# One 128-column stationary operand for the two halves of v, and an add by VectorE

## The chip, the cores and the metric

The kernel runs on one core of one Trainium2 chip. The metric is the device time of one execution in microseconds; the figure quoted for a kernel is the median of its runs.

## The reference, cut to what matters

Two transformer blocks run one after the other on 512 tokens of width 1024. The change touches the second block alone: a mixer with four groups of four attention heads of width 64 (A, dilated causal; B, stick-breaking; C, a band of 128 with sinks, two heads of values shared by four of queries; D, causal over blocks), and a cross attention of four heads over 256 memory tokens. In all of them the output of a head is a product of a weight matrix with that head's values:

```python
# softmax heads (A, C, D and cross attention), for each head:
p = exp(score + bias - max) / denominator
y = p @ v                       # v: keys x 64
# stick-breaking heads (B): p comes from sigmoids and a running sum of softplus, y = p @ v as well
```

## The kernel before, in words

Activations lie transposed, features on the 128 partitions and the tokens along a row. A product of two float32 matrices is made from float32r halves: each operand is split into a high half (a ScalarE copy) and a low half (a VectorE subtraction), and three matmuls are accumulated, high by high, high by low and low by high (`split`, `mm3`).

`hybrid` runs the mixer. Its list `plan` pairs the heads of a group (`heads`, `band_heads`) with jobs that fill TensorE meanwhile: the projections of the next groups (`pair`, `values`) and the output projection (`project_out`). `weave` starts one generator per tile of 128 queries and moves all running ones one step on, then emits some of the fill. The order within each engine's queue is set when the program is built, from simulated times of the instructions (`schedule_with_timeline_sim=True`); each engine then runs its queue in that order. The plan goes B, A, D, C; `cross` follows with the same softmax generators and its own fill.

A softmax generator (`softmax_units`, `unit`) handles 128 queries: two score matmuls (line 1206) into a bank `sc`, minimum or maximum and exponential, normalisation, transposes of the weights by TensorE (line 1228) into a bank `tr`, and their split into pth and ptl, which hold two query tiles side by side, 256 columns. After the second tile of a pair come the products with v (lines 1250 to 1254): for each block of 128 keys that both tiles see one block of 256 columns, for the others one of 128 columns; three matmuls each, whose stationary operand is the 64 columns of one head in v's high or low half (tiles v2h, v2l; xv in cross attention). They fill rows 0 to 63 of a `tr` bank, and ScalarE copies these to the head's rows of y, rows 0 to 63 or 64 to 127.

A stick-breaking generator (`stick_units`) handles 128 keys and all later queries, so its products (line 1307) have 512, 384, 256 and 128 columns; four generators of a head accumulate in one `tr` bank, copied at the end (line 1310).

There are three `tr` banks, shared by transposes, half of the stick-breaking scores and these outputs.

The values come from `values` (line 1418; groups A, B and D by tiles of 128 tokens, group C by transposing a projection) and, for cross attention, from `memory_keys` (line 1598) early in the kernel; that one writes its halves to HBM (`mvd`) over SP's queue, and `memory_load` (line 1642) fetches them on GpSimd's queue at the start of `cross`.

Of the kernel before, what the change touches and what calls it, by code (L numbers as in the profile page):

```python
# [63 lines left out]
class Net:  # L64
# [1114 lines left out]
            out.append((kh, kl))  # L1179
        return out  # L1180

    def softmax_units(self, q, ks, v, vc, y, yr, window, bias=None, sink=None, keys=SEQ, tag=lambda pair: pair,
                      again=False):

        nc = self.nc
        V = nc.vector
        vh, vl = v
        nkt = keys // P  # L1190
        st = {}

        def unit(ti):
            pair, i = divmod(ti, 2)
            wins = [window(2 * pair + n) for n in range(2)]
            k0, k1 = wins[i]
            f0 = wins[0][0]
            w = (k1 - k0) * P
            if bias is not None and (ti == 0 or again and i == 0):
                st["e"] = self.bt.tile([P, 512], FT, name="bias")  # L1200
                nc.sync.dma_start(st["e"], bias)
            ps = self.psc.tile([P, 512], FT, name="sc")
            qs, q0 = q(pair)
            qs = qs[:, q0 + i * P:q0 + i * P + P]
            for x in range(2):
                nc.tensor.matmul(ps[:, 0:w], qs, ks[x][:, k0 * P:k1 * P], start=x == 0, stop=x == 1)
            p = self.at.tile([P, keys], FT, name="e")[:, 0:w]
            nm, den = (self.at.tile([P, 1], FT, name=n) for n in ("nm", "den"))
            if bias is not None:
                o = 384 - P * ti + P * k0  # L1210
                V.tensor_tensor_reduce(p, ps[:, 0:w], st["e"][:, o:o + w], -1.0, 3.0e38 if sink is None else sink[1],
                                       OP.add, OP.min, nm)
            else:
                V.tensor_reduce(nm, ps[:, 0:w], AX.X, OP.max, negate=True)
                nc.scalar.activation(p, ps[:, 0:w], AF.Exp, bias=nm, accum_out=den)
            yield
            if bias is not None:
                nc.scalar.activation(p, p, AF.Exp, scale=-1.0, bias=nm, accum_out=den)
            if sink is not None:
                e = self.at.tile([P, 1], FT, name="es")  # L1220
                nc.scalar.activation(e, sink[0], AF.Exp, bias=nm)
                V.tensor_tensor(den, den, e, OP.add)
            V.reciprocal(den, den)
            V.tensor_scalar(p, p, den, None, OP.mult)
            yield
            pt = self.ptr.tile([P, 512], FT, name="tr")
            for j in range(k1 - k0):
                nc.tensor.transpose(pt[:, j * P:(j + 1) * P], p[:, j * P:(j + 1) * P], self.ident)
            yield
            if i == 0:  # L1230
                n = wins[1][1] - f0
                k = tag(pair)
                full = 1280 if k and keys == SEQ else 512
# [12 lines left out]
            both = [j for j in range(nkt) if a0 <= j < a1 and b0 <= j < b1]  # L1246
            jobs = [(j, 0, 256) for j in both]
            jobs += [(j, 0, P) for j in range(a0, a1) if j not in both]
            jobs += [(j, P, 256) for j in range(b0, b1) if j not in both]
            for ji, (j, c0, c1) in enumerate(jobs):  # L1250
                for x, (m, d) in enumerate(((vh, pth), (vh, ptl), (vl, pth))):
                    nc.tensor.matmul(yp[0:64, c0:c1], m[:, j, vc:vc + 64], d[:, j - f0, c0:c1], start=ji == x == 0,
                                     stop=ji == len(jobs) - 1 and x == 2)
            nc.scalar.activation(y[yr, pair * 256:pair * 256 + 256], yp[0:64, 0:256], AF.Copy)

        return [unit(i) for i in range(4)]

    def stick_units(self, q, ks, v, vc, y, yr):


        nc = self.nc
        V, G = nc.vector, nc.gpsimd
        vh, vl = v
        st = {}

        def unit(i):
# [36 lines left out]
            if i == 3:  # L1303
                st["y"] = self.ptr.tile([P, 512], FT, name="tr")
            yp = st["y"]
            for x, (m, d) in enumerate(((vh, ah), (vh, al), (vl, ah))):
                nc.tensor.matmul(yp[0:64, t0:SEQ], m[:, i, vc:vc + 64], d, start=i == 3 and x == 0,
                                 stop=i == 0 and x == 2, skip_group_check=True)
            if i == 0:
                nc.scalar.activation(y[yr], yp[0:64], AF.Copy)  # L1310

        return [unit(i) for i in (3, 2, 1, 0)]

# [28 lines left out]
    def hybrid(self):  # L1342
# [3 lines left out]
        with ExitStack() as es:  # L1346
# [65 lines left out]

            def new_v(name):
                pool = self.vx if name == "D" else self.vp
                boxes[name]["v"] = tuple(pool.tile([P, 4, 256], FR, name=n) for n in ("v2h", "v2l"))
                return boxes[name]["v"]

            def values(name):

                if name == "C":  # L1420
                    def then(vf):
                        vh, vl = new_v("C")
                        pt = self.ptr.tile([P, 512], FT, name="tr")
                        for j in range(4):
                            nc.tensor.transpose(pt[:, j * P:(j + 1) * P], vf[:, j * P:(j + 1) * P], self.ident)
                        self.split(vh[:, :, 0:P], vl[:, :, 0:P], pt.rearrange("p (a b) -> p a b", a=4))
                    return pair(15, 1.0, then)
                ws = []

# [3 lines left out]
                                           ready=self.ready.get(("v", "ABD".index(name), c))) for c in range(2))  # L1433

                def tile_(t):
                    vh, vl = boxes[name]["v"]
                    ps = self.pmm.tile([P, 512], FT, name="mm")
                    sl = slice(NM + t * P, NM + t * P + P)
                    self.mm3(ps[:, 0:256], [(self.xh[k][:, sl], self.xl[k][:, sl], ws[k // 4][0][:, k % 4, :],
                                             ws[k // 4][1][:, k % 4, :]) for k in range(KT)])  # L1440
                    col = self.rcol[HALF[t // 2][0]]
                    self.split(vh[:, t, :], vl[:, t, :], ps[:, 0:256], col[:, t % 2:t % 2 + 1])
                return load, [lambda t=t: tile_(t) for t in range(4)]

            def finish(g):
# [31 lines left out]
            def heads(name, j):  # L1477
                def gens():
# [5 lines left out]
                    for i in range(2):  # L1484
                        h = 2 * j + i
                        y, yr, q = ys[2 * g + j], slice(64 * i, 64 * i + 64), box["q", j][i]
                        if name == "B":
                            yield from self.stick_units(q, box["k", j][i], box["v"], 64 * h, y, yr)
                            continue
                        e = self.bias_tile({"A": 0, "D": 8}[name] + h)  # L1490
                        yield from self.softmax_units(lambda pair, q=q: (q, 256 * pair), box["k", j][i], box["v"],
                                                      64 * h, y, yr, causal, e)
                return gens

            def band_heads(pair):

                box = boxes["C"]
                if pair == 0:
                    for j in range(2):
                        ys[4 + j] = bt.tile([P, SEQ], FT, name="qkn")  # L1500
                    for h in range(4):
                        j, i = divmod(h, 2)
                        q = box["q", j][i]
                        box["u", h] = self.softmax_units(
                            lambda pair, q=q: (q, 256 * pair), box["k", 0][j], box["v"], 64 * j, ys[4 + j],
                            slice(64 * i, 64 * i + 64), band, self.bias_tile(4 + h),
                            (self.par[:, sk + h:sk + h + 1], nsink[:, h:h + 1]),
                            tag=lambda pair, h=h: 1 if pair else h % 2, again=True)
# [89 lines left out]
    def memory_keys(self, mp):  # L1598
# [2 lines left out]
        nc = self.nc  # L1601
        mh, ml, rm = self.mem
        self.mkd = self.dram.tile([P, 8, MEM], FT, name="mkd")
        self.mvd = self.dram.tile([P, 4, 256], FT, name="mvd")

        def keys(f):
            st = {}
# [14 lines left out]
                            nc.sync.dma_start(self.mkd[o:o + 64, 4 * f + 2 * j + x],  # L1622
                                              ks[x][64 * j:64 * j + 64].bitcast(FT))
            return load, [make]
        v = [mp.tile([P, 2, 256], FR, name=n) for n in ("vh", "vl")]
        ws = []

        def load():
# [2 lines left out]
        def values(t):  # L1631
# [1 line left out]
            sl = slice(t * P, t * P + P)  # L1633
            self.mm3(ps[:, 0:256], [(mh[k][:, sl], ml[k][:, sl], ws[k // 4][0][:, k % 4, :],
                                     ws[k // 4][1][:, k % 4, :]) for k in range(KT)])
            self.split(v[0][:, t, :], v[1][:, t, :], ps[:, 0:256], self.mcol[:, t:t + 1])
            if t == 1:
                for i in range(2):
                    nc.sync.dma_start(self.mvd[:, 2 * i:2 * i + 2], v[i].bitcast(FT))
        return [keys(0), keys(1), (load, [lambda t=t: values(t) for t in range(2)])]  # L1640

    def memory_load(self, pool):

        k = pool.tile([P, 8, MEM], FR, name="xk")
        v = pool.tile([P, 4, 256], FR, name="xv")
        self.nc.gpsimd.dma_start(k, self.mkd)
        self.nc.gpsimd.dma_start(v, self.mvd)
        return [(k[:, 2 * h], k[:, 2 * h + 1]) for h in range(4)], (v[:, 0:2], v[:, 2:4])

    def cross(self, es, out):  # L1650

# [83 lines left out]
        units = []  # L1735
        for h in range(4):
            q = lambda pair, h=h: (qs[HALF[pair][0], h // 2][h % 2], 0)
            units.append(self.softmax_units(q, kss[h], v, 64 * h, o[h // 2], slice(64 * (h % 2), 64 * (h % 2) + 64),
                                            lambda i: (0, 2), keys=MEM, tag=lambda pair, h=h: h % 2))
        by_pair = [[units[h][2 * pair + i] for h in range(4) for i in range(2)] for pair in range(2)]  # L1740

# [230 lines left out]
```

## Time and profile before

| | |
|---|---|
| median of 3 runs | 1524.08 us (1523.75 to 1529.01) |
| profiled execution, its own time | 1525.71 us |
| its span, first to last instruction | 1524.0 us |
| TensorE busy | 1464.5 us, 96% |
| VectorE busy | 1007.3 us, 66% |
| ScalarE busy | 741.2 us, 49% |
| mean granted TensorE clock, share of full speed | 0.994 |

TensorE's busy time is the union of its matmuls, whose ends are modelled and overlap the next ones, so a busy TensorE isn't one at its peak: the distance between the starts of two matmuls tells more than the duration of one. PEld is the loading of weights, which runs beside the matmuls. Where a line with x8 is given, eight instructions are merged; its time is then that of all of them.

### The profile page before, as it was taken

The numbers are of one execution on the slowest core, as the hardware profiler recorded it, in microseconds if no ns is written. First come the engines' busy times: TensorE is split into PE (matmuls) and PEld (weight loads), VectorE is DVE, ScalarE is ACT, GpSimd is POOL, SyncE is SP. The second block draws the span as 40 slices with busy tenths as digits, with TensorE's granted clock in tenths as the row PEclk, the third lists the DMA queues.
The fourth block names the chain that finished last, engine by engine and source line by source line (L and its number), as shares of the span: only waits on it lengthen the run. The fifth ranks groups of instructions, "written<-read, shape, count | busy, mean of one in ns | idle before, by whom it ended". The sixth has DMA issues, their size and how long they took to land.

```text
span 1524.0 us, 25154 instructions
## 1 busy us (share of the span) xinstructions
PE 1464.5 (96%) x9769; PEld 1319.5 (87%) x9769; DVE 1007.3 (66%) x1963; ACT 741.2 (49%) x1437; POOL 284.0 (19%) x321
## 2 busy tenths in 40 slices
PE   7899899999989999999999999999989999999996
PEld 7899899988989999989999988988888888888886
DVE  6988979878587766665474755888896443344334
ACT  5333356655665444444454465686685431144321
POOL 1157821003352111100131211000221000000001
PEclk9999999999999999999999999999999999999998
DMA  6333342226546766643657244314211322233221
GB/s 207 100 100 98 103 114 89 65 69 225 162 140 221 255 229 245 226 136 110 184 155 237 99 152 140 124 43 146 97 57 56 97 96 93 88 98 97 97 83 56
DMA packets 76223, 197.63 MB, mean 130 GB/s; under 512 B 16188, under 2 KB 25644, under 8 KB 75976
## 3 DMA queue, kind: packets, MB, share of 16 engines
q1 hardware_dynamic: 67384, 166.66, 34.9%
q0 software_dynamic: 7632, 28.31, 4.9%
q8 instruction: 77, 1.26, 0.3%
q10 hardware_dynamic: 1088, 1.05, 0.2%
q14 instruction: 42, 0.34, 0.1%
HBM read 171.75 MB, written 28.15 MB: 131 GB/s over the span
## 4 chain that ended last, share of the span: by engine, by line
PE 65%; DVE 7%; ACT 3%; DMA 2%; issue 1%; DVEq 0%; SPq 0%; ACTq 0%
PE mm L146 6%; PE mm L147 6%; PE mm L149 6%; PE mm L176 5%; PE mm L179 5%; PE mm L178 5%; PE mx L176 4%; PE mx L179 4%; PE mx L178 4%; PE mx L146 3%; PE mx L147 3%; PE mx L149 3%; PE mm L1396 2%; PE mm L1395 2%; PE mm L1393 2%; DVE xl L109 1%
## 5 line engine op out<-in xcount | busy, mean ns | idle before, releaser
L127 DVE TENSOR_TENSOR wlo<-wst,whi 128x1024 fp32r<-128x1024 f32 (+3 forms) x244 | 299.2, 1228 | 193.1 <-ACT whi L126 116.9
L126 ACT ACTIVATE whi<-wst 128x1024 fp32r<-128x1024 f32 (+3 forms) x244 | 249.9, 1026 | 283.6 <-PE mm L147 113.8
L178 PE MATMUL mm<-xh,whi 128*128 128x256 f32 (+4 forms) x800 | 229.2, 312 | 3.0 <-DVE vl L109 1.6
L179 PE MATMUL mm<-xl,whi 128*128 128x256 f32 (+4 forms) x800 | 229.6, 313 | 0.2
L178 PE MATMUL mx<-xh,whi 128*128 128x512 f32 (+3 forms) x576 | 174.2, 325 | 8.2 <-ACT xh L108 8.2
L179 PE MATMUL mx<-xl,whi 128*128 128x512 f32 (+3 forms) x576 | 175.0, 326 | 1.3 <-DVE xl L109 1.2
L178 PEld LDWEIGHTS mm<-xh,whi 128*128 128x128 f32 (+1 forms) x800 | 150.6, 188 | 13.0 <-DVE vl L109 1.8
L179 PEld LDWEIGHTS mm<-xl,whi 128*128 128x128 f32 (+1 forms) x800 | 150.2, 188 | 10.5 <-issue 0.6
L176 PE MATMUL mm<-xh,wlo 128*128 128x256 f32 (+4 forms) x800 | 138.2, 312 | 0.0
L146 PE MATMUL mm<-hh,whi 128*128 128x256 f32 (+1 forms) x480 | 132.6, 307 | 0.0
L147 PE MATMUL mm<-hl,whi 128*128 128x256 f32 (+1 forms) x480 | 132.5, 307 | 0.0
L178 PEld LDWEIGHTS mx<-xh,whi 128*128 128x128 f32 x576 | 109.2, 190 | 17.1 <-ACT xh L108 8.5
L176 PEld LDWEIGHTS mm<-xh,wlo 128*128 128x128 f32 (+1 forms) x800 | 115.3, 187 | 9.9 <-issue 0.4
L179 PEld LDWEIGHTS mx<-xl,whi 128*128 128x128 f32 x576 | 108.8, 189 | 11.9 <-DVE xl L109 2.8
L176 PE MATMUL mx<-xh,wlo 128*128 128x512 f32 (+3 forms) x576 | 104.3, 322 | 0.0
L146 PEld LDWEIGHTS mm<-hh,whi 128*128 128x128 f32 x480 | 90.4, 189 | 5.4
L147 PEld LDWEIGHTS mm<-hl,whi 128*128 128x128 f32 x480 | 90.5, 189 | 5.1
L176 PEld LDWEIGHTS mx<-xh,wlo 128*128 128x128 f32 x576 | 86.0, 187 | 9.1
L252 POOL TENSOR_TENSOR nacc<-nacc,sq 128x256 f32<-128x256 f32 (+2 forms) x58 | 56.2, 970 | 202.2 <-ACT sq L251 193.0
L149 PE MATMUL mm<-hh,wlo 128*128 128x256 f32 (+1 forms) x480 | 79.5, 307 | 1.3 <-DVE wlo L127 1.3
L149 PEld LDWEIGHTS mm<-hh,wlo 128*128 128x128 f32 x480 | 67.5, 188 | 6.7 <-DVE wlo L127 1.7
L252 POOL TENSOR_TENSOR acc<-acc,sq 128x264 f32<-128x264 f32 (+1 forms) x6 | 4.3, 741 | 335.3 <-ACT sq L251 335.3
(570 smaller groups left out, 3305.7 us busy)
## 6 DMA issues: line engine op xcount, KB each, us to landing
wst<-in_w_in_dram SPq DMA_DIRECT2D x39, 512.0 KB, 3.5
wst<-in_w_down_dram SPq DMA_DIRECT2D x32, 512.0 KB, 3.5
wst<-in_w_mup_dram SPq DMA_DIRECT2D x32, 512.0 KB, 3.5
wst<-in_w_mdown_dram SPq DMA_DIRECT2D x32, 512.0 KB, 3.7
wst<-in_w_gate_dram SPq DMA_DIRECT2D x22, 512.0 KB, 4.0
wst<-in_w_up_dram SPq DMA_DIRECT2D x22, 512.0 KB, 3.5
wst<-in_w_out_dram SPq DMA_DIRECT2D x20, 512.0 KB, 3.9
ready<-phi POOLq DMA_DIRECT2D x17, 512.0 KB, 3.1
```

The lines of the kernel that those rows point to most:

```text
L126: nc.scalar.activation(hi[:, 0:n], st[:, 0:n], AF.Copy)
L127: nc.vector.tensor_tensor(lo[:, 0:n], st[:, 0:n], hi[:, 0:n].bitcast(FT), OP.subtract)
L146: nc.tensor.matmul(ps, ah, bh, start=start and i == 0, stop=False)
L147: nc.tensor.matmul(ps, ah, bl, start=False, stop=False)
L149: nc.tensor.matmul(ps, al, bh, start=False, stop=stop and i == n - 1)
L176: nc.tensor.matmul(ps, wl[:, k], xh, start=False, stop=k == KT - 1)
L178: nc.tensor.matmul(ps, wh[:, k], xh, start=k == 0, stop=False)
L179: nc.tensor.matmul(ps, wh[:, k], xl, start=False, stop=False)
L252: (nc.vector if k % len(accs) else nc.gpsimd).tensor_tensor(acc[:, c:c + w], acc[:, c:c + w], sq, OP.add)
L1393: nc.tensor.matmul(ps, wl[:, k], xh, start=False, stop=k == KT - 1)
L1395: nc.tensor.matmul(ps, wh[:, k], xh, start=k == 0, stop=False)
L1396: nc.tensor.matmul(ps, wh[:, k], xl, start=False, stop=False)
```

## The change

The halves of v of one head lie side by side, [high 64 | low 64], as one tile `v2` (in cross attention one tile `v` and `xv`). One matmul with this 128-column operand gives rows 0 to 63 with the high half and rows 64 to 127 with the low half, so that a block needs two matmuls, by pth and by ptl, and the product of the two low halves comes in too. In the softmax heads this holds for the blocks of 256 columns; those of 128 columns keep three matmuls with 64-column operands, in rows 0 to 63. In the stick-breaking heads it holds for all blocks. `add_halves` then evicts: ScalarE copies the row half that lies on the other partitions than y's to y, and VectorE adds the other row half, from PSUM, in place.

Group C's values are split in two halves of two strided runs each in place of one; the other splits write with a stride. `memory_keys` sends one transfer per tile of 128 memory tokens, where it sent one per half after the second tile.

```diff
-        vh, vl = v
+        vh, vl = self.v_halves(v)
...
             for ji, (j, c0, c1) in enumerate(jobs):
-                for x, (m, d) in enumerate(((vh, pth), (vh, ptl), (vl, pth))):
-                    nc.tensor.matmul(yp[0:64, c0:c1], m[:, j, vc:vc + 64], d[:, j - f0, c0:c1], start=ji == x == 0,
-                                     stop=ji == len(jobs) - 1 and x == 2)
-            nc.scalar.activation(y[yr, pair * 256:pair * 256 + 256], yp[0:64, 0:256], AF.Copy)
+                cols = slice(c0, c1)
+                if ji < len(both):
+                    terms = [(v[:, j, head], d) for d in (pth, ptl)]
+                else:
+                    terms = [(vh[:, j, head], pth), (vh[:, j, head], ptl), (vl[:, j, head], pth)]
+                for x, (m, d) in enumerate(terms):
+                    nc.tensor.matmul(yp[0:m.shape[-1], cols], m, d[:, j - f0, cols], start=ji == x == 0,
+                                     stop=ji == len(jobs) - 1 and x == len(terms) - 1, skip_group_check=True)
+            self.add_halves(y[yr, pair * 256:pair * 256 + 256], yr, yp[:, 0:256])
...
+    def v_halves(self, v):
+
+        return [v[:, :, :, 64 * x:64 * x + 64] for x in range(2)]
+
+    def add_halves(self, y, yr, ps):
+
+        here, there = (slice(64 * x, 64 * x + 64) for x in ((0, 1) if yr.start == 0 else (1, 0)))
+        self.nc.scalar.activation(y, ps[there], AF.Copy)
+        self.nc.vector.tensor_tensor(y, y, ps[here], OP.add)
...
-            for x, (m, d) in enumerate(((vh, ah), (vh, al), (vl, ah))):
-                nc.tensor.matmul(yp[0:64, t0:SEQ], m[:, i, vc:vc + 64], d, start=i == 3 and x == 0,
-                                 stop=i == 0 and x == 2, skip_group_check=True)
+            for x, d in enumerate((ah, al)):
+                nc.tensor.matmul(yp[:, t0:SEQ], v[:, i, head], d, start=i == 3 and x == 0, stop=i == 0 and x == 1,
+                                 skip_group_check=True)
             if i == 0:
-                nc.scalar.activation(y[yr], yp[0:64], AF.Copy)
+                self.add_halves(y[yr], yr, yp)
...
-                boxes[name]["v"] = tuple(pool.tile([P, 4, 256], FR, name=n) for n in ("v2h", "v2l"))
-                return boxes[name]["v"]
+                boxes[name]["v"] = pool.tile([P, 4, 4, P], FR, name="v2")
+                return self.v_halves(boxes[name]["v"])
...
-                        self.split(vh[:, :, 0:P], vl[:, :, 0:P], pt.rearrange("p (a b) -> p a b", a=4))
+                        for h in range(2):
+                            self.split(vh[:, :, h], vl[:, :, h], pt.rearrange("p (a h c) -> p h a c", a=4, h=2)[:, h])
...
-                    self.split(vh[:, t, :], vl[:, t, :], ps[:, 0:256], col[:, t % 2:t % 2 + 1])
+                    self.split(vh[:, t], vl[:, t], ps[:, 0:256].rearrange("p (h c) -> p h c", h=4), col[:, t % 2:t % 2 + 1])
...
-            self.split(v[0][:, t, :], v[1][:, t, :], ps[:, 0:256], self.mcol[:, t:t + 1])
-            if t == 1:
-                for i in range(2):
-                    nc.sync.dma_start(self.mvd[:, 2 * i:2 * i + 2], v[i].bitcast(FT))
+            self.split(vh[:, t], vl[:, t], ps[:, 0:256].rearrange("p (h c) -> p h c", h=4), self.mcol[:, t:t + 1])
+            nc.sync.dma_start(self.mvd[:, t], v[:, t].bitcast(FT))
```

## Rows read from the trace of the kernel before

**Rows 1.** The page, part 1: busy us (share of the span), instructions, by engine.
```profile
PE 1464.5 (96%) x9769; PEld 1319.5 (87%) x9769; DVE 1007.3 (66%) x1963; ACT 741.2 (49%) x1437; POOL 284.0 (19%) x321
```

**Rows 2.** Lines 1252 and 1307: count, ns min/median/max, first and last start, forms.
```profile
L1252 PE MATMUL tr<-pth,v2h x68: 220/277/362, 975.1 to 1079.4; 128*64 128x256 f32 x40, 128*64 128x128 f32 x28
...
L1252 PE MATMUL tr<-pth,xv x32: 274/280/362, 1114.7 to 1148.4; 128*64 128x256 f32 x32
...
L1307 PE MATMUL tr<-pth,v2h x16: 222/309/421, 889.8 to 968.5; 128*64 128x128 f32 x4, 128*64 128x256 f32 x4, 128*64 128x384 f32 x4, 128*64 128x512 f32 x4
```

**Rows 3.** Busy times by stretch, from 895 to 1150 us.
```profile
core 0: us, PE busy (x) PEld busy (x) DVE busy (x) ACT busy (x) POOL busy (x), PEclk, DMA share, GB/s
895.00:972.00 77.00, 77.00 (x442) 66.69 (x441) 51.68 (x123) 46.71 (x115) 13.49 (x26) 1.00 0.40 131
...
1000.00:1035.00 35.00, 33.22 (x241) 28.81 (x240) 33.35 (x114) 29.06 (x82) 0.00 (x0) 1.00 0.15 45
...
1058.00:1082.00 24.00, 20.50 (x166) 17.64 (x165) 20.78 (x75) 18.66 (x61) 0.74 (x1) 1.00 0.20 67
...
1117.00:1150.00 33.00, 29.37 (x226) 26.31 (x224) 27.59 (x87) 24.07 (x76) 5.35 (x7) 1.00 0.09 32
```

**Rows 4.** The chain of waits from 895 to 972 us, shares by line.
```profile
by line: PE mm L1393 19.7%; PE mm L1395 18.4%; PE mm L1396 18.2%; PE tr L1307 8.9%; PE tr L1289 8.2%; PE mm L146 5.1%; PE mm L149 5.0%; PE mm L147 4.9%; PE sc L1289 4.1%; PE tr L1275 2.5%; PE sc L1206 2.2%; PE sc L1275 1.8%; PE rs L290 0.9%
```

**Rows 5.** The chain of waits, 890 to 1165 us, pieces: start, us on it, what.
```profile
941.15 1.17 PE mm L1393 x5
...
955.28 0.95 PE mm L149 x8
...
969.56 0.46 PE tr L1307 x2
...
976.07 0.46 PE tr L1228 x4
...
1022.80 0.60 ACT v2h L105
```

**Rows 6.** TensorE in order of time, 981.8 to 982.2 us: start, duration, line, operands.
```profile
981.80 0.28 PE L1206 MATMUL sc<-kh,qs 128*128 128x256 f32 x1
981.92 0.28 PE L1252 MATMUL tr<-pth,v2h 128*64 128x256 f32 x1
982.03 0.28 PE L1206 MATMUL sc<-kl,qs 128*128 128x256 f32 x1
982.15 0.39 PE L1396 MATMUL mm<-xl,whi 128*128 128x512 f32 x1
```

**Rows 7.** TensorE in order of time, 983.6 to 983.8 us, a block of 128 columns.
```profile
983.67 0.22 PE L1252 MATMUL tr<-pth,v2h 128*64 128x128 f32 x1
...
983.79 0.22 PE L1252 MATMUL tr<-pth,v2l 128*64 128x128 f32 x1
```

**Rows 8.** VectorE's groups by shape, 860 to 1165 us: busy us, mean ns, idle before.
```profile
L1683 DVE TENSOR_TENSOR x<-x,mm 128x256 f32<-128x256 f32 x16 | 6.6, 412 | 1.1 <-PE mm L149 1.0
...
L1524 DVE TENSOR_TENSOR x<-x,mm 128x512 f32<-128x512 f32 x8 | 5.5, 683 | 0.7 <-PE mm L149 0.7
```

**Rows 9.** VectorE in order of time, two subtractions back to back in group C.
```profile
1075.21 0.75 DVE L106 TENSOR_TENSOR ptl<-tr,pth 128x256 fp32r<-128x256 f32 x2
```

**Rows 10.** Line 1254, the copies of the softmax heads' outputs, columns as in rows 2.
```profile
L1254 ACT ACTIVATE y<-tr x16: 358/376/380, 977.0 to 1054.3; 64x256 f32<-64x256 f32 x16
L1254 ACT ACTIVATE qkn<-tr x8: 375/377/378, 1059.6 to 1080.5; 64x256 f32<-64x256 f32 x8
L1254 ACT ACTIVATE o<-tr x8: 357/376/384, 1118.3 to 1148.7; 64x256 f32<-64x256 f32 x8
```

**Rows 11.** Line 1254 alone in one stretch: length, ScalarE's busy us (count), clock, DMA.
```profile
1000.00:1035.00 35.00, 3.02 (x8) 1.00 0.15 45
```

**Rows 12.** Waits of weight loading, 895 to 1160 us: in total, times, longest.
```profile
PEld tr L1228 <- ACT y L1254: 0.6, 1, 0.6
```

**Rows 13.** TensorE's first output product after cross attention's last head; idle before it.
```profile
1150.15 0.50 PE L146 MATMUL mm<-oh,whi 128*128 128x256 f32 x2 [0.80 <-ACT oh L105]
```

**Rows 14.** SP's queue near 465 us, the last transfer of the memory values.
```profile
465.51 0.33 SPq L1639 DMA_DIRECT2D mvd<-vl x1
```

More of the change, by code (lines that the diff above doesn't have):

```diff
@@ L1180, in stack_k, with softmax_units @@
         return out
-    def softmax_units(self, q, ks, v, vc, y, yr, window, bias=None, sink=None, keys=SEQ, tag=lambda pair: pair,
+    def softmax_units(self, q, ks, v, head, y, yr, window, bias=None, sink=None, keys=SEQ, tag=lambda pair: pair,
                       again=False):
@@ L1250, in unit, with stick_units @@
             for ji, (j, c0, c1) in enumerate(jobs):
-                for x, (m, d) in enumerate(((vh, pth), (vh, ptl), (vl, pth))):
-                    nc.tensor.matmul(yp[0:64, c0:c1], m[:, j, vc:vc + 64], d[:, j - f0, c0:c1], start=ji == x == 0,
-                                     stop=ji == len(jobs) - 1 and x == 2)
-            nc.scalar.activation(y[yr, pair * 256:pair * 256 + 256], yp[0:64, 0:256], AF.Copy)
-        return [unit(i) for i in range(4)]
-    def stick_units(self, q, ks, v, vc, y, yr):
+                cols = slice(c0, c1)
[7 more added lines that the diff above has]
+            self.add_halves(y[yr, pair * 256:pair * 256 + 256], yr, yp[:, 0:256])
+        return [unit(i) for i in range(4)]
+    def v_halves(self, v):
[4 more added lines that the diff above has]
+        self.nc.vector.tensor_tensor(y, y, ps[here], OP.add)
+    def stick_units(self, q, ks, v, head, y, yr):
         nc = self.nc
         V, G = nc.vector, nc.gpsimd
-        vh, vl = v
         st = {}
@@ L1435, in tile_ @@
                 def tile_(t):
-                    vh, vl = boxes[name]["v"]
+                    vh, vl = self.v_halves(boxes[name]["v"])
                     ps = self.pmm.tile([P, 512], FT, name="mm")
@@ L1487, in gens @@
                         if name == "B":
-                            yield from self.stick_units(q, box["k", j][i], box["v"], 64 * h, y, yr)
+                            yield from self.stick_units(q, box["k", j][i], box["v"], h, y, yr)
                             continue
@@ L1491, in gens @@
                         yield from self.softmax_units(lambda pair, q=q: (q, 256 * pair), box["k", j][i], box["v"],
-                                                      64 * h, y, yr, causal, e)
+                                                      h, y, yr, causal, e)
                 return gens
@@ L1504, in band_heads @@
                         box["u", h] = self.softmax_units(
-                            lambda pair, q=q: (q, 256 * pair), box["k", 0][j], box["v"], 64 * j, ys[4 + j],
+                            lambda pair, q=q: (q, 256 * pair), box["k", 0][j], box["v"], j, ys[4 + j],
                             slice(64 * i, 64 * i + 64), band, self.bias_tile(4 + h),
@@ L1603, in memory_keys @@
         self.mkd = self.dram.tile([P, 8, MEM], FT, name="mkd")
-        self.mvd = self.dram.tile([P, 4, 256], FT, name="mvd")
+        self.mvd = self.dram.tile([P, 2, 4, P], FT, name="mvd")
         def keys(f):
@@ L1624, in keys @@
             return load, [make]
-        v = [mp.tile([P, 2, 256], FR, name=n) for n in ("vh", "vl")]
+        v = mp.tile([P, 2, 4, P], FR, name="v")
+        vh, vl = self.v_halves(v)
         ws = []
@@ L1644, in memory_load @@
         k = pool.tile([P, 8, MEM], FR, name="xk")
-        v = pool.tile([P, 4, 256], FR, name="xv")
+        v = pool.tile([P, 2, 4, P], FR, name="xv")
         self.nc.gpsimd.dma_start(k, self.mkd)
         self.nc.gpsimd.dma_start(v, self.mvd)
-        return [(k[:, 2 * h], k[:, 2 * h + 1]) for h in range(4)], (v[:, 0:2], v[:, 2:4])
+        return [(k[:, 2 * h], k[:, 2 * h + 1]) for h in range(4)], v
     def cross(self, es, out):
@@ L1737, in cross @@
             q = lambda pair, h=h: (qs[HALF[pair][0], h // 2][h % 2], 0)
-            units.append(self.softmax_units(q, kss[h], v, 64 * h, o[h // 2], slice(64 * (h % 2), 64 * (h % 2) + 64),
+            units.append(self.softmax_units(q, kss[h], v, h, o[h // 2], slice(64 * (h % 2), 64 * (h % 2) + 64),
                                             lambda i: (0, 2), keys=MEM, tag=lambda pair, h=h: h % 2))
```

## Prediction

> **What bounds the kernel now.** I read the page's first part first: TensorE is busy for 96% of the span, VectorE for 66% [rows 1]. An average says little of one stage, so next I asked where the changed lines run. The products of weights and values (line 1252 for the softmax heads, 1307 for stick-breaking) lie between 889 and 1149 us [rows 2]; all else of the change is one transfer near 460 us. Third, busy times by stage over that part [rows 3]. Two kinds of stage show. From 895 to 972 (group B) TensorE is busy throughout and VectorE for 52 of 77 us. In three dense stages TensorE has gaps and VectorE is nearly as full as it: 1000 to 1035 (end of A, most of D), 1058 to 1082 (C), 1117 to 1150 (cross attention). Fourth, the chain of waits: for 895 to 972 every listed entry is TensorE [rows 4], so a matmul less there is time saved. In the dense stages the chain also passes through ScalarE and VectorE; one such piece is in [rows 5].
>
> **What it removes.** A matmul's own duration overlaps its neighbours', so I price by distance between starts. In the chain, eight 256-column matmuls with a 128-column weight take 0.95 us, 0.119 each; five of 512 columns take 1.17, 0.234 each; two of 512 with a 64-column weight 0.46, 0.23 each [rows 5]. Between 64-column and 128-column weights at 256 moving columns the starts are 0.12, 0.11 and 0.12 apart [rows 6]. So a 256-column matmul costs 0.117 whether its weight has 64 or 128 columns; a 384-column one, halfway, 0.175. With 128 moving columns the weight does matter: three matmuls with 64 columns start 0.06 apart [rows 7], four transposes, whose loaded operand has 128 columns, take 0.46, 0.115 each [rows 5]. That is where the doubled weight is not hidden, and the change keeps the three-term form for those blocks in the softmax heads.
>
> Softmax heads: 40 of the 68 column blocks in groups A, C and D are 256 wide; the 32 cross-attention products with the high half or the low half on pth are 16 pairs, so 16 blocks more [rows 2]. Each loses one matmul of three: 56 x 0.117 = 6.55 us. Stick-breaking: 16 blocks, four of each width [rows 2]. Per head it loses 0.117 + 0.175 + 0.234 = 0.53, and at the 128-wide block pays 2 x 0.115 in place of 3 x 0.06, 0.05 more: 0.48 a head, 1.9 us. Together TensorE is freed of 6.55 + 1.9 = 8.4 us. If all of it reached the end it would be 0.55% of the span; a measurement of this kernel tells about 0.5% (7.6 us) from no change, so "faster" needs nearly the whole sum.
>
> **What it adds.** Each of 36 evictions gets a VectorE add behind ScalarE's copy, whose size and engine stay: 32 of 64x256 and 4 of 64x512. The nearest rows are VectorE's adds of a PSUM operand to an SBUF one over 128 partitions, 0.41 us at 256 columns and 0.68 at 512 [rows 8]; in a full queue two 256-column operations end 0.75 after the first starts, so one occupies 0.34 more [rows 9]. Where it lies:
> - B: 4 x 0.68 = 2.7 us on a VectorE with 25 us free [rows 3]: nothing. Without that cover it would cost up to 2.7.
> - From 972 to 1000 and 1035 to 1058, 8 adds: taken at nothing, since the dense stretches lie elsewhere; at most 8 x 0.34 = 2.7.
> - The dense stages: 8 of the 16 group A and D copies run from 1000 to 1035, 8 in C, 8 in cross attention [rows 3, 10, 11]. 24 x 0.34 = 8.2 us enters VectorE's queue, which has 1.6, 3.2 and 5.4 us free there, 10.3 together, in pieces that are partly waits for its inputs. The adds stand in order with the softmax steps on which TensorE's next scores and transposes wait. Between nothing (each falls in a gap) and 24 x 0.70 = 16.8 (each delays TensorE by itself and one operation ahead of it), I take half the added work, 4.1 us: VectorE is full in the first, and the chain is only partly its own in the others.
> - The tr bank, one of three, is held until the add has read it, not the copy. Today transposes wait on the copy now and then, 0.6 us in the longest listed [rows 12]; the same 4.1 and the same ends cover it.
> - Two exposed ends, where cross attention's last copy leads to the split and TensorE waits for it (0.80 us idle before 1150.15) [rows 13], and likewise after C: 2 x 0.41 = 0.8 us.
>
> **Small edits.** C's value split becomes two pairs of 256 columns in place of one of 512. The one ScalarE piece of 0.60 us at 1022.8 lies on the chain [rows 5]; two of the 0.38 of a copy [rows 10] are 0.15 more, on VectorE 2 x 0.41 - 0.68 [rows 8] is 0.14 more: 0 to 0.3, inside the rounding. The values written with a stride: same elements per instruction; VectorE's ptl writes, also into slices, take what the adds take [rows 8, 9], so nothing. The memory values' transfers: on SP's queue both wait today for the second tile's split, the last at 465.5 [rows 14]; now the first needs only the first tile's halves, and the last leaves where the last does today. The weight loads queued behind both go no later than before: nothing, with 0.3 (one issue of that row) either way. Loads of 128-column weights behind a 128-column matmul: at most 0.06 a run, 2 us over 32 runs, taken at 0, since most runs stand among 256-column or wider matmuls.
>
> The order of instructions on each engine is made anew when the program is built, so an edit can move neighbours too. Bounds: the gaps of TensorE in the three dense stages, 1.8 + 3.5 + 3.6 = 8.9 us [rows 3], won or doubled; no row gives a sign, so 0.
>
> **Sum.** -8.4 + 4.1 + 0.8 = -3.5 us. The profiled execution took 1525.71 us, span 1524.0 and 1.7 around it; it would take 1522.2. The median of the runs is 1524.08, 1.6 lower, so the forecast is 1524.1 - 3.5 = 1520.6.
>
> **The rivals.**
> A, the cover holds: the adds fall in gaps and the whole 8.4 arrives, 1515.7. For it: 10.3 us free on VectorE against 8.2 needed; TensorE is the longest part of the chain. Against: in the first dense stage 1.6 us are free for 2.7.
> B, even: VectorE's added 8.2 us delay TensorE one for one, plus the 0.8: 1524.1 - 8.4 + 9.0 = 1524.7.
> C, the other side: a bank held through ScalarE's copy, VectorE's queue and the add keeps TensorE's transposes waiting. Place: the 24 dense evictions; price 0.70 each; 16.8 + 0.8 - 8.4 = +9.2, 1533.3. It decides against the change from 7.6 / 24 = 0.32 us per eviction on, and beyond the bound of measurement from 0.63. For it: full queues and three banks; against: the longest of today's listed waits on that bank is 0.6 us, once [rows 12].
> D, a switch between 64- and 128-column weights empties the array. The matmuls would start a whole duration apart, 0.28 in place of 0.117. There are 48 runs of 64-column products now (24 in A, C and D, 8 in cross attention, 16 stick blocks) with two switches each; stick and cross lose theirs, 48 x 0.16 = 7.7 us more, 1512.9. Rows speak against it: the starts stay 0.12 apart across the switch [rows 6]. The Trainium skill, TensorEngine Tiling (Array Packing), section Key Properties, says that a change of tiling mode drains the TensorE; by that rule the sum would be -11.2, by the row -3.5, and I go by the row.
> That 128-column products stream slower, and it doesn't save what it says, is excluded by [rows 5].
>
> **How the numbers follow.** Forecast (take-back from 1 to 8 us, 1517 to 1523.5) 0.52; A 0.16; B 0.18; C 0.11; D 0.03. Likeliest: 1520.6. The range 1514 to 1531 takes in A, the forecast, B and most of a rebuilt order; outside lie C, D and some 0.05 of a larger reordering, 0.19. Faster by over 0.5% (under 1516.5): D and, since A lies only 0.8 under that line, somewhat over half of A, 0.12. Slower (over 1531.7): C, 0.11. Within: 0.77.
>
> **What would show it.** Right: 72 matmuls fewer (56 and 16); stage B shorter by some 1.9 us with TensorE still gapless; VectorE 13 to 16 us busier, above all from 1000 to 1150; the add at 0.41; new idle time of TensorE behind transposes that wait for the add. The first step is wrong if blocks of 256 columns start more than 0.13 apart; the take-back is wrong if the dense stages shrink by the full 0.117 per block, or if they grow. The whole would be wrong if time appears or goes outside 889 to 1150, which would be the order made anew.

## The result, and the profile after

The changed kernel takes 1538.5 us (median of 6 runs, 1536.45 to 1539.48) against 1524.22 us for the kernel before on the same chip (6 runs): ratio 1.009, 95% interval 1.0078 to 1.0102. It is slower by 14.3 us; the forecast was 3.5 us faster, and the time lies outside the range. The profiled execution took 1539.43 us, its span is 1537.7 us, the mean granted clock 0.986 (0.994 before).

The page's first part, as [rows 1]:

```profile
PE 1472.7 (96%) x9697; PEld 1325.7 (86%) x9697; DVE 1021.0 (66%) x2000; ACT 745.9 (49%) x1438; POOL 284.6 (19%) x321
```

There are 72 matmuls fewer, as promised, and yet TensorE is busy for 8.2 us more. VectorE has 13.7 us more. The matmul lines, now 1257 (softmax) and 1321 (stick-breaking), as [rows 2]: count, shortest/median/longest, first and last start, forms.

```profile
L1257 PE MATMUL tr<-pth,v x96: 220/279/581, 974.1 to 1092.8; 128*64 128x128 f32 x56, 128*128 128x256 f32 x40
L1257 PE MATMUL tr<-pth,xv x16: 279/282/384, 1127.6 to 1162.0; 128*128 128x256 f32 x16
L1321 PE MATMUL tr<-pth,v x16: 222/308/401, 889.6 to 966.5; 128*128 128x128 f32 x4, 128*128 128x256 f32 x4, 128*128 128x384 f32 x4, 128*128 128x512 f32 x4
```

The medians are those of before. New is the longest, 581 ns for the form that took at most 362 before. The first stick-breaking product starts at 889.6 us (889.8 before), so nothing was lost ahead of it, and from cross attention's end on the two traces run at a constant distance. All of the loss lies between 889 and 1163 us. Busy times by stretch, as [rows 3] (the column after POOL is the granted clock):

```profile
895.00:972.00 77.00, 76.12 (x431) 66.80 (x430) 53.31 (x128) 47.79 (x116) 12.97 (x26) 1.00 0.42 134
1000.00:1035.00 35.00, 29.70 (x175) 24.96 (x175) 32.69 (x108) 25.77 (x72) 0.00 (x0) 0.85 0.12 36
1058.00:1082.00 24.00, 19.86 (x116) 16.24 (x114) 20.31 (x74) 16.54 (x56) 0.00 (x0) 0.86 0.33 104
1082.00:1117.00 35.00, 31.70 (x231) 29.49 (x232) 29.57 (x73) 21.79 (x55) 8.10 (x10) 0.90 0.32 106
1117.00:1150.00 33.00, 28.97 (x222) 26.44 (x221) 32.04 (x93) 27.91 (x82) 8.38 (x10) 1.00 0.21 65
```

In the first dense stage TensorE is busy for 3.5 us less and issues 175 matmuls where 241 stood, although the change takes only some 13 of them away (8 of the 24 evictions that share 40 blocks); the clock is 0.85, 0.86 and 0.90 where it was 1.00. How that begins is seen at 1002 us. TensorE in order of time (start, duration, line, operands, idle before and who ended it):

```profile
1002.31 0.60 PE L1228 MATMUL tr<-ident,e 128*128 128x128 f32 x4
1004.14 0.50 PE L1206 MATMUL sc<-kh,qs 128*128 128x512 f32 x1 [1.23 <-DVE nm L1211]
...
1006.26 0.35 PE L1257 MATMUL tr<-pth,v 128*128 128x256 f32 x1 [1.21 <-DVE y L1271]
1006.77 0.58 PE L1257 MATMUL tr<-ptl,v 128*128 128x256 f32 x1 [0.15 <-DVE ptl L106]
1007.15 0.42 PE L1257 MATMUL tr<-pth,v 128*128 128x256 f32 x1
1007.37 0.41 PE L1257 MATMUL tr<-ptl,v 128*128 128x256 f32 x1
...
1014.97 0.28 PE L1257 MATMUL tr<-pth,v 128*128 128x256 f32 x1
1015.09 0.28 PE L1257 MATMUL tr<-ptl,v 128*128 128x256 f32 x1
1015.20 0.22 PE L1257 MATMUL tr<-pth,v 128*64 128x128 f32 x1
1015.26 0.22 PE L1257 MATMUL tr<-ptl,v 128*64 128x128 f32 x1
```

ScalarE in order of time, the copy of the eviction that TensorE waits for:

```profile
1003.66 0.38 ACT L1270 ACTIVATE y<-tr 64x256 f32<-64x256 f32 x1
```

VectorE in order of time, behind it:

```profile
1004.00 0.55 DVE L1211 CUSTOM_DVE_ANT_0 e<-sc,bias 128x384 f32<-128x384 f32 x1
1004.48 0.08 DVE L1211 DVE_READ_ACCUMULATOR2_ANT nm<- 128x1 f32 x1
...
1004.67 0.42 DVE L1178 CAST kl<-kl 64x512 fp32r<-64x512 f32 x1
1005.10 0.69 DVE L1412 SCALAR_TENSOR_TENSOR qkn<-mm,rs 128x512 f32<-128x512 f32 x1
1005.71 0.40 DVE L1271 TENSOR_TENSOR y<-y,tr 64x256 f32<-64x256 f32 x1
```

ScalarE's copy was done at 1004.04. The add behind it starts 1.67 us later, since VectorE's queue stood full; only then does the bank come free and TensorE, idle for 1.21 us, goes on. The clock in the next stretches:

```profile
1004.00:1006.00 2.00, 0.92 (x4) 0.60 (x4) 1.96 (x8) 1.98 (x10) 0.00 (x0) 1.00 0.00 0
1006.00:1008.00 2.00, 1.58 (x6) 1.42 (x7) 1.97 (x8) 0.61 (x3) 0.00 (x0) 0.65 0.00 0
1008.00:1010.00 2.00, 1.85 (x10) 1.45 (x10) 1.85 (x9) 1.11 (x3) 0.00 (x0) 0.50 0.00 0
1010.00:1012.00 2.00, 2.00 (x12) 2.00 (x13) 1.93 (x10) 1.60 (x6) 0.00 (x0) 0.50 0.51 135
1014.00:1016.00 2.00, 2.00 (x20) 1.92 (x18) 1.76 (x6) 1.74 (x5) 0.00 (x0) 1.00 0.00 0
```

After the two gaps the granted clock is at the lower of its two levels (0.50 of full speed, 1.2 of 2.4 GHz) for 6 to 7 us; 256-column matmuls then start 0.21 to 0.22 us apart (1007.15, 1007.37), at full clock 0.12 or 0.11 (1014.97, 1015.09, 1015.20). The same returns three times up to 1117 us, from 1030, 1068 and 1085 us on. The adds themselves (busy us, mean ns, idle before), as [rows 8], and the waits for them (in total, times, longest), as [rows 12]:

```profile
L1271 DVE TENSOR_TENSOR y<-y,tr 64x256 f32<-64x256 f32 x16 | 6.7, 417 | 2.4 <-ACT y L1270 2.1
L1271 DVE TENSOR_TENSOR y<-y,tr 64x512 f32<-64x512 f32 x4 | 2.7, 686 | 0.6 <-ACT y L1270 0.5
```

```profile
PE sc L1206 <- DVE nm L1211: 3.8, 5, 1.3
PE tr L1228 <- DVE qkn L1271: 1.6, 2, 0.9
PE tr L1257 <- DVE y L1271: 1.2, 1, 1.2
```

With two shorter ones (0.6 and 0.4) the listed waits for the add come to 3.8 us of TensorE, the waits for the running minimum, which stands in the same VectorE queue, to 3.8 (1.5 before, longest 0.5). That is not 14 us, so the experiments had to find the rest.

### The profile page after: what moved, and what is told of

Same layout as the page of the kernel before. It is cut to its first block, busy times and chain, and to the rows that moved or that the text cites. A ratio compares the mean times of both kernels' runs of the same rounds, so it can differ in the third digit from the quotient of the medians.

```text
span 1537.7 us, 25107 instructions
## 1 busy us (share of the span) xinstructions
PE 1472.7 (96%) x9697; PEld 1325.7 (86%) x9697; DVE 1021.0 (66%) x2000; ACT 745.9 (49%) x1438; POOL 284.6 (19%) x321
## 4 chain that ended last, share of the span: by engine, by line
PE 62%; DVE 10%; DMA 2%; ACT 2%; issue 1%; SPq 0%; POOL 0%; DVEq 0%; ACTq 0%; POOLq 0%
PE mm L146 6%; PE mm L147 6%; PE mm L149 6%; PE mm L176 5%; PE mm L179 5%; PE mm L178 5%; PE mx L176 4%; PE mx L179 4%; PE mx L178 4%; PE mx L146 3%; PE mx L147 3%; PE mx L149 2%; DVE xl L109 2%; PE mm L1410 2%; PE mm L1409 2%; PE mm L1407 2%
```

## The experiments

The order of the instructions on each engine is made anew at each build. Against before, 816 of the 9451 matmuls that both kernels have stand elsewhere in TensorE's queue (by up to 36 places), and 332 of 1915 VectorE instructions. Several kernels below are therefore "held to an order": every common instruction of an engine follows the one that it followed in the named kernel (a dependence without a semaphore), and only what is new is placed by the build.

```diff
+        for a, b in zip(queue, queue[1:]):      # queue: the engine's instructions in the other kernel's order
+            tc.add_manual_dep(b, a.name, mybir.DependencyInfo(mybir.DependencyClass.NoSync, ...))
```

All runs in one table. Some traces reach group B's start up to 4 us early or late, by stretches that no edit touches. So besides the ratio of the medians it has a second reading of the profiled run: its span less the start of the first stick-breaking product, against the same of before, 1524.0 - 889.8 = 634.2 us.

| kernel | median us | ratio to before, 95% | from B's start to the end, against before | clock |
|---|---|---|---|---|
| the change | 1538.5 | 1.0078 to 1.0102 | +13.8 | 0.986 |
| e1 change without adds | 1521.97 | 0.9966 to 0.9988 | -3.3 | 0.992 |
| e13 the same, before's order | 1520.81 | 0.9963 to 0.9983 | -3.9 | 0.994 |
| e9 change, before's order | 1534.52 | 1.0049 to 1.0078 | +9.6 | 0.988 |
| e12 group B only, before's order | 1524.73 | 0.9989 to 1.0010 | -1.75 | 0.995 |
| e5 group B only | 1528.8 | 1.0011 to 1.0037 | +1.1 | 0.994 |
| e10 before, the change's order | 1537.28 | 1.0074 to 1.0102 | +11.3 | 0.989 |
| e2 before, a second copy | 1537.67 | 1.0064 to 1.0101 | +10.0 | 0.992 |
| e8 before, extra VectorE work | 1538.02 | 1.0063 to 1.0101 | +11.2 | 0.991 |
| e11 the same, before's order | 1539.62 | 1.0082 to 1.0116 | +15.7 | 0.987 |
| e3 two copies, add in SBUF | 1532.78 | 1.0030 to 1.0065 | +7.2 | 0.990 |
| e4 the same, add by GpSimd | 1537.38 | 1.0055 to 1.0100 | +11.8 | 0.990 |
| e6 before, program order | 1581.85 | 1.0347 to 1.0389 | | |
| e7 change, program order | 1577.87 | 1.0323 to 1.0361 | | |
| e14 change with spare matmuls | 1534.82 | 1.0049 to 1.0088 | +11.8 | 0.989 |
| e16 before with spare matmuls | 1529.18 | 1.0013 to 1.0036 | +4.3 | 0.996 |

**The two halves of the change.** First the matmuls without the add (the output then lacks the product with v's low half), and the eviction's added work without the matmuls.

```diff
-        self.nc.scalar.activation(y, ps[there], AF.Copy)
-        self.nc.vector.tensor_tensor(y, y, ps[here], OP.add)
+        self.nc.scalar.activation(y, ps[0:64], AF.Copy)              # e1, in the change
...
             nc.scalar.activation(y[yr, pair * 256:pair * 256 + 256], yp[0:64, 0:256], AF.Copy)
+            V.tensor_copy(y[yr, pair * 256:pair * 256 + 256], yp[0:64, 0:256])   # e2, in before
```

> The matmul part alone: 72 matmuls fewer, ScalarE copies rows 0 to 63 of the bank (the high half's rows), VectorE adds nothing; so the products with the low half of v are left out in the 128-column blocks. Theory H (the add behind the copy, by holding the tr bank and queueing on VectorE, makes the gaps in which TensorE falls to its lower clock level): the gain of the matmuls arrives, 1516 to 1519 us, and the granted clock is back at 0.993 or more. Theory R (the order that the build makes anew is what cost the 14 us, the add has little to do with it): 1530 to 1540.

> The other part alone: the kernel before with its 64-column matmuls, and behind each of the 36 copies by ScalarE a VectorE copy of the same rows from the same bank to the same y, as long in the bank and nearly as long on VectorE as the add. Theory H: slower than before by 14 to 22 us, 1538 to 1546, with the clock under 0.99 (the add's price without the matmuls' 8). Theory R: 1520 to 1529, unless this order is unlucky too.

e1 takes 3.5 us less than before: of the 8.4 us that the matmuls were to bring, under half arrives even with nothing added. e2 takes 12.2 us more without one matmul changed. The loss hangs on the eviction, the matmuls bring little; which part of the eviction, and whether the new order has a hand in both, isn't told by these two.

**Group B alone**, where VectorE has room: the softmax heads keep three matmuls and one copy.

```diff
-                if ji < len(both):
+                if False:
...
-            self.add_halves(y[yr, pair * 256:pair * 256 + 256], yr, yp[:, 0:256])
+            nc.scalar.activation(y[yr, pair * 256:pair * 256 + 256], yp[0:64, 0:256], AF.Copy)
```

> The new layout of v, but 128-column products and the add in the stick-breaking group B alone; all softmax heads keep three 64-column matmuls and ScalarE's copy. Stage B is bound by TensorE and VectorE has room there, so both theories of the add expect nearly the whole of B's 1.9 us: 1521.5 to 1524 against 1524.5 to 1525.5 of before. If a new order alone costs time, anything from 1520 to 1535.

> 128-column products and the add in group B alone, bound to the order of the kernel before. In an order of its own it was 0.24% slower than before. Theory R: B's 1.9 us arrive, 0.9975 to 0.9995 of before. Theory H: as in its own order, 1.001 to 1.004.

With the order of its own build this part, too, loses 3.9 us by the medians (from B's start on 1.1). Held to before's order it gains 1.75 us from B's start on in the profiled run; the medians (0.5 us more than before, the interval from 1.7 less to 1.5 more) can't be told from no change.

```profile
L1321 PE MATMUL tr<-pth,v x16: 222/336/476, 889.4 to 966.5; 128*128 128x128 f32 x4, 128*128 128x256 f32 x4, 128*128 128x384 f32 x4, 128*128 128x512 f32 x4
```

The span of that trace is 1521.9 us, the last of these starts is 2.0 us earlier than in [rows 2] and the first 0.4.

**The held bank or VectorE's queue?** In e3 both row halves of the softmax heads leave the bank by ScalarE copies and VectorE adds from SBUF; e4 gives that add to GpSimd. e8 does the opposite: VectorE gets the extra work, in SBUF and behind the copy, so that no bank is held for it.

```diff
-        self.nc.vector.tensor_tensor(y, y, ps[here], OP.add)
+        self.nc.scalar.activation(t, ps[here], AF.Copy)
+        self.nc.vector.tensor_tensor(y, y, t, OP.add)                 # e3; self.nc.gpsimd in e4
...
+            V.tensor_tensor(yc, yc, yc, OP.max)                       # e8, in before, yc: the copied rows of y
```

> The change, but in the 32 softmax evictions ScalarE copies both row halves out of the bank (0.38 us more on ScalarE each) and VectorE adds them in SBUF: the bank is free after ScalarE, VectorE's work stays. If the held bank is the price (H1): 1518 to 1526. If VectorE's fuller queue is the price (H2): 1534 to 1544, as the change or a little above.

> As the kernel with two copies, but GpSimd adds: the bank is free after ScalarE and VectorE has no added work in the softmax heads. H1 and H2 both: 1516 to 1524. R: 1530 to 1540. If ScalarE's 32 further copies (12 us) are a bound of their own: 1526 to 1532.

> The kernel before, and behind each of the 36 copies VectorE works on y in SBUF (y = max(y, y), the same shapes): VectorE's queue gets the same load and the same place as the add, the bank is free after ScalarE. If the held bank is the price (H1): 1526 to 1530. If the queue is (H2): 1534 to 1540, as the kernel with the copy behind. Half and half lies between.

> The kernel before with VectorE's added work in SBUF behind each copy, bound to the order of the kernel before. It took 1538.0 in an order of its own. Theory R: 1523 to 1530. Theory H (queue): 1534 to 1540 again.

e8 and e11 lose 13 and 15 us with the banks released as before: a held bank isn't needed for the loss. 36 instructions on VectorE, nearly all of 0.4 to 0.7 us, are enough (0.42 at the median for the 32 of 256 columns in e8), in either order. e3 gives back 7 us of the change's 14 while VectorE keeps its adds, outside what either theory expected; it may be the bank's share. That isn't shown, since e3 has an order of its own, and two orders of one kernel lie 1 to 4 us apart by the medians (the change and e9, e5 and e12, e1 and e13, e8 and e11). e4 takes the add off VectorE and still loses 11.9, where both theories expected none: work on ScalarE, the longer way of y (0.73 us for an add by GpSimd) or the new order cost as well, and can't be told apart here.

**The order.**

```diff
-    with _tile.TileContext(nc, schedule_with_timeline_sim=True) as tc:
+    with _tile.TileContext(nc, schedule_with_timeline_sim=False) as tc:
```

> The kernel before with the instructions of each engine in the order in which the program emits them, not ordered by simulated times. Base for the next run; itself probably slower than before, 1530 to 1600. No theory says how much.

> The change in the order in which the program emits its instructions, so that nothing else moves against the run of before in program order. Theory H (the add's wait): slower than that one by 5 to 20 us. Theory R (the cost came from the order made anew): 0 to 8 us faster than that one.

> The change, with every engine bound to issue its instructions in the order that the build made for the kernel before; only the 36 adds and the second half of C's value split are placed by the build. Theory R (the order made anew is the price): 1516 to 1525. Theory H (the add's work and the wait behind it are the price): 1533 to 1542. Between the two, 1526 to 1532, each has a share.

> The kernel before, nothing of the change, bound to the order that the build made for the change (the 72 matmuls that the change lacks are placed by the build). Theory R: 1530 to 1542, though not one instruction is added. Theory H: 1520 to 1529.

In program order both are slower by over 50 us; the change isn't slower than before there (4.0 us less, intervals that overlap), so the loss shows only in the interleaved order. e9: before's order takes 4 us off the change, and 10 stay. e10: the change's order, laid on the kernel before, costs 13 us with nothing added. Were the order the whole cause, e9 would be back at before's time or under it; it isn't. An order made for other work says little about what the order costs in the changed kernel itself; 14.3 - 10.3 = 4.0 us is that.

**What was still open**: does the rest of the 8.4 us arrive if the order is held, and is the lower clock a cause or a companion? e13 is e1 held to before's order. e14 and e16 add 48 matmuls on data that are there, into a bank that nobody reads, ahead of the transposes of D, C and cross attention.

```diff
+                spare = self.pmm.tile([P, 512], FT, name="rs", bufs=1)
+                nc.tensor.matmul(spare[:, 0:keys], qs, ks[0][:, 0:keys], start=True, stop=True)
                 pt = self.ptr.tile([P, 512], FT, name="tr")
```

> The change without its adds (ScalarE copies the high half's rows alone, so the low half of v is left out), every engine held to the order of the kernel before. Theory, two limits: where TensorE is full the 72 matmuls come off one for one, in the dense stages VectorE ends the waits and they bring little, whatever the order: 0.9965 to 0.999 (-1.5 to -5 us), as with the order of the build (0.9977). Rival, the order made anew ate the rest of the 8.4 us: 0.9945 (-8.4), all stages from 1000 to 1150 shorter by 0.117 for each matmul.

> The change, with one matmul more ahead of the transposes of each 128 queries in D, C and cross attention, on operands that are there already and into a bank that nobody reads: 48 matmuls, 32 of 512 and 16 of 256 columns, by the rows 32 x 0.234 + 16 x 0.117 = 9.4 us of TensorE. If the lower clock after the gaps is the greater part of the loss, these fill gaps, the granted clock of 1000 to 1117 stays nearer 1.00 (0.85, 0.86 and 0.90 in the change) and the time falls under the change's 1.0094 in spite of the added work, to 1.000 to 1.006. If the waits themselves are the loss and the clock only goes along, 1.009 to 1.016.

> The same 48 spare matmuls in the kernel before, whose clock is at 1.00 there already: what the spare work itself costs, with an order made anew. If it fits the gaps 1.000, if it is paid in full 1.006; the order made anew can add up to 0.009 more, as it did when the kernel before was held to the changed kernel's order.

e13 settles the first: -3.9 us from B's start on (e1 -3.3), so the missing gain is not the order's. It also gives the pair that was wanted, since e13 and e9 have one order and differ by the adds alone (and by which rows ScalarE copies). Their dense stretches, e13 first:

```profile
1000.00:1035.00 35.00, 31.81 (x221) 27.68 (x220) 32.03 (x112) 26.83 (x79) 0.00 (x0) 1.00 0.20 54
1058.00:1082.00 24.00, 21.09 (x158) 18.87 (x159) 20.28 (x60) 19.40 (x54) 3.36 (x4) 0.93 0.15 41
1082.00:1117.00 35.00, 33.30 (x264) 31.43 (x262) 31.57 (x82) 23.61 (x65) 10.44 (x13) 1.00 0.40 132
1117.00:1150.00 33.00, 29.26 (x208) 25.72 (x208) 27.85 (x79) 23.87 (x73) 8.68 (x11) 1.00 0.06 16
```

e9:

```profile
1000.00:1035.00 35.00, 28.59 (x186) 24.73 (x185) 31.45 (x109) 24.59 (x70) 0.00 (x0) 0.90 0.13 33
1058.00:1082.00 24.00, 17.59 (x110) 14.68 (x108) 22.13 (x79) 17.26 (x57) 0.00 (x0) 0.86 0.25 80
1082.00:1117.00 35.00, 33.70 (x262) 32.31 (x263) 29.29 (x64) 22.91 (x57) 10.49 (x13) 0.95 0.33 109
1117.00:1150.00 33.00, 28.60 (x205) 26.06 (x204) 31.23 (x95) 25.72 (x78) 7.95 (x9) 0.95 0.19 61
```

The waits for the add in e9, 895 to 1165 us (in total, times, longest):

```profile
PE tr L1228 <- DVE qkn L1271: 3.7, 3, 1.6
PE tr L1257 <- DVE y L1271: 2.0, 2, 1.6
```

The adds bring waits for them (5.7 us listed, up to 1.6 each) and a clock of 0.86 to 0.95, where e13 has 1.00 but for one stretch of 0.93.

The held traces can also be cut at the same instructions: from the first to the 25th of TensorE's transposes of the softmax weights (line 1228), and from there to the last. Before, e13, e9, and the second part of e11:

```profile
963.27:997.65 34.38, 34.38 (x211) 29.98 (x210) 26.20 (x83) 20.93 (x55) 0.00 (x0) 1.00 0.39 131
997.65:1144.75 147.10, 136.76 (x995) 121.21 (x994) 131.52 (x402) 110.25 (x319) 18.45 (x23) 1.00 0.27 87
957.87:991.01 33.14, 33.14 (x202) 29.16 (x201) 25.46 (x80) 20.69 (x55) 0.00 (x0) 1.00 0.41 136
991.01:1137.19 146.18, 134.17 (x948) 119.20 (x947) 131.16 (x404) 110.12 (x318) 19.16 (x23) 0.99 0.28 87
961.33:994.47 33.14, 33.14 (x202) 29.16 (x201) 27.18 (x84) 21.17 (x55) 0.00 (x0) 1.00 0.42 136
994.47:1154.06 159.59, 140.03 (x949) 125.27 (x947) 142.19 (x431) 111.85 (x318) 19.16 (x23) 0.94 0.26 80
996.76:1159.63 162.87, 146.57 (x995) 130.22 (x994) 142.34 (x429) 110.79 (x319) 18.48 (x23) 0.93 0.25 78
```

In the first part, where TensorE is never idle, e9 is as fast as e13 to 0.01 us, though adds run there and in B: they cost nothing. In the second e9 takes 13.4 us longer with the same matmuls: TensorE is idle for 7.5 us more (19.6 against 12.0) and busy for 5.9 more. e11 against before: 15.8 longer, 6.0 more idle, 9.8 more busy. Busy times rest on modelled ends, so these shares are rough, but neither the waits nor the slower matmuls make up the loss alone.

e14 came to 1.0068, between the two cases. Its dense stretches:

```profile
1000.00:1035.00 35.00, 33.56 (x217) 28.64 (x216) 31.67 (x108) 26.43 (x72) 0.00 (x0) 0.95 0.11 31
1058.00:1082.00 24.00, 20.72 (x129) 16.93 (x127) 21.22 (x75) 17.20 (x56) 0.00 (x0) 0.93 0.30 99
1082.00:1117.00 35.00, 32.95 (x238) 30.25 (x237) 28.40 (x67) 22.10 (x54) 9.25 (x11) 0.90 0.33 106
1117.00:1150.00 33.00, 30.60 (x225) 28.38 (x224) 30.40 (x88) 25.43 (x75) 7.73 (x9) 0.95 0.21 65
```

9.4 us of useless TensorE work did not make the change slower: against before on its own chip its loss falls from 14.3 to 9.2 us, with intervals that overlap, while in the kernel before the same work costs 3.5. That leans to the clock as a cause and isn't proof: each build also had a new order.

## Why the prediction was wrong

Three comparisons take the sum apart. They are differences of the last-but-one column, so each rests on profiled runs; the medians, each against before on its own chip, stand in brackets.

| term | predicted us | measured us | from |
|---|---|---|---|
| 72 matmuls less | -8.4 | -3.9 (-4.8) | e13 |
| of these, group B | -1.9 | -1.75 (+0.5) | e12 |
| of these, softmax heads | -6.55 | -2.1 (-5.3) | e13 less e12 |
| adds, bank and exposed ends | +4.9 | +13.4 (+15.1) | e9 less e13 |
| order made anew | 0 | +4.3 (+4.0) | the change less e9 |
| sum | -3.5 | +13.8 (+14.3) | |

The medians bear out the three main terms. How the 3.9 divide between B and the softmax heads is shown by the traces alone.

- **Prices of matmuls: right.** The starts 0.12 apart with a 128-column operand in the change (1014.97 to 1015.09) are those of [rows 6]; group B's 1.9 us came as 1.75 in e12's trace. Rival D is out: from 128-column to 64-column weights and on, the starts at 1015.09, 1015.20 and 1015.26 lie 0.11 and 0.06 apart.
- **"Each loses one matmul of three: 56 x 0.117 = 6.55 us", as a gain at the end: wrong by two thirds in the traces.** From the first to the 25th transpose, where TensorE is full, e13 needs 1.24 us less than before with 9 matmuls fewer (33.14 against 34.38). From there to the last, through all dense stages, it gains only 0.9 with 47 fewer (146.18 against 147.10): TensorE is busy for 2.6 us less and idle for 1.7 more, and e13 has up to 1.7 us of lower clock there that before has not. The text had named those stages as ones where VectorE is nearly as full [rows 3], halved the cost of the adds on that ground, and yet counted the gain in full. A matmul taken out of a queue that waits for VectorE mostly lengthens the wait.
- **"I take half the added work, 4.1 us": wrong, and the step that fails most.** The adds have the size and length foreseen (0.41 and 0.69 us) and VectorE's 13.7 more busy us were foreseen as 13 to 16. But they cost 13.4 us, even where the order is held. The 7 that run ahead of the 25th transpose cost nothing, so the other 29 cost 0.46 us each, at 0.42 long. The bounds of 0 to 16.8 held it; the choice inside them did not. The free time of 1.6, 3.2 and 5.4 us was no cover: at 1004 us the add stands behind work that VectorE has to do anyway, and TensorE waits for both.
- **The lower clock: not in the sum at all.** In [rows 3] every stretch is at 1.00, and no step asked what happens if a gap there grows. Added up from the stretches, time times (1 - clock) is 0.15 x 35 + 0.14 x 24 + 0.10 x 35 = 12.1 us in the change, 10.3 in e9, 1.7 in e13, 0 before. The Trainium skill, TensorE: Matmul & The Clock Gate, section Terms, prices time at the reduced clock at about this product; by it, as an estimate, 8.6 of the adds' 13.4 us would be the clock's. The traces have less: the same matmuls keep TensorE busy for 5.9 us more in e9 than in e13, and the rest, 7.5, is idle time. e2 and e8 lose 10.0 and 11.2 us with about 5 by that product, and e8 is at 1.00 up to 1082 us. Whether the lower clock would have come without the longer waits, no run tells.
- **The order, taken at 0 and bounded by 8.9: the bound held for the change (+4.3), not for what an order can do** (e10, +11.3 from B's start on). Without the adds, the order of the build costs little (e1 less e13: 0.6, by the medians 1.3), so the 4.3 belongs to the two together. In e8 and e11 it is the build's own order that loses less, so there is no fixed sign.
- **Rival C** (1533.3) had the sign and came nearest, with "a bank held through ScalarE's copy, VectorE's queue and the add": the trace shows such a wait at 1004 to 1006 us, of a product with v. But its cause is not whole: e11 loses as much with no bank held.
- **The small edits** cost nothing that shows: B starts at 889.6 us against 889.8 before, so the memory values' transfers moved nothing, and e12, which has the new layout with all its splits, can't be told from before.

Left open: whether the lower clock is a cause of its own, how much of the change's loss is the held bank, how much of e4 is ScalarE's second copy, and what a better order for the change would give. With no adds at all, in before's order, e13 gains 3.9 us, 0.3% of the kernel.

## What to carry to other kernels

Price a gain and a cost by the same rule: in a stage whose waits end at VectorE, matmuls taken away are worth little (0.9 us for 47) and a VectorE instruction put in can cost its whole length and more (0.46 us for 0.42), however the average busy share of 66% reads; where TensorE is never idle and VectorE has room, the same instruction cost nothing. Where a stage runs at full clock with TensorE waiting now and then, a longer wait can be paid twice, once as idle time and once at the lower clock behind it (7.5 and 5.9 us here). To judge an edit in a kernel whose order is made at build time, hold the order, change one thing and compare the two traces between the same instructions; laying the new order on the old kernel says little.

## What the runs showed of the hardware that was not expected

- Two idle times of TensorE of 1.23 and 1.21 us, with a few matmuls between, were followed by 6 to 7 us at half of full clock, in which 256-column matmuls started 0.21 us apart in place of 0.117; the kernel before has idle times of 0.73 to 0.90 us in its dense stages (six up to 1150.15 us) and 1.00 throughout. The length of one idle time doesn't decide it: in e8 two of 1.34 and 0.88 us, 2 us apart (at 1009.13 and 1011.17), and in e13 one of 1.54 (at 1019.06) were followed by none.
- 48 matmuls more, 9.4 us of TensorE at full clock, in a kernel that had lost clock: no slower (1.0068 against 1.009), with the clock of the first dense stage at 0.95 in place of 0.85.
